# Attention of a head stage by stage for both halves, and the meta products of the next group in front of the present second quad, in a float32 convolution-and-retention trunk

## The chip, the cores and the metric

The kernel runs on one core of a Trainium2 chip. The metric is the device time of one execution in microseconds (us). The engines are TensorE (PE, matrix products into PSUM), VectorE (DVE), ScalarE (ACT), GpSimd (POOL) and SyncE (SP, which here issues all transfers between HBM and SBUF). Each engine runs its own queue in order; semaphores tie the queues together.

## The reference

One layer over 2048 tokens of width 1024, with 16 learned meta tokens ahead of them. Batch is 1, and all data is float32.

```python
hn = rms_norm(concat(meta, x), norm1_g)
cx, cb, cc, cg, q, k, v, rg = split(hn @ w_in, 8)          # 8 parts of 512 columns
conv_out = cb * causal_conv(cc * cx, conv_w) * silu(cg)    # 3 taps for each column
qf, kf = rotary(q) * 128 ** -0.5, rotary(k)                # 4 heads of 128 columns
ret = retention_chunkwise(qf, kf, v)                       # chunks of 128 tokens, a decayed state per head
ret_out = head_group_norm(ret, ret_norm_g) * silu(rg)
out = rms_norm(x + concat(conv_out, ret_out) @ w_out, final_g)   # the meta tokens' rows are dropped
```

In each head `retention_chunkwise` makes, chunk by chunk, the masked scores `q k^T` times `v` plus `q` times the state before the chunk, and updates the state with the decayed `k^T v`. The meta tokens matter in two ways alone: their `k` and `v` give each head's first state, and their `cc * cx` the two values that the convolution needs from before the first token.

## The kernel before

Work is laid out with columns of the projection on partitions and tokens along the free axis. The tokens are taken in two **rounds** (r) of 1024, each of two **halves** (j) of 512. Within a round come four heads (h), each a K,V group and a Q,RG group of projections, and then four convolution groups (g), each a CC,CX group and a CG,CB group. A group of projections is a **quad**: 2 x 2 blocks of output over the two halves and two blocks of the contraction. A quad is made in the Strassen-Winograd way with seven block products (L199 to L234). A float32 operand is split into a high and a low part (`wh`, `wl` for weights, `mh`, `ml` for tokens), and each block product is three times four matmuls 128x512 (L208), so a quad has 84 big products on PE. The first quads of a round and of the output are plain ones of 96 (L258). `take` then combines the banks on DVE and does what the group needs (rotation, gates).

The weights of a quad come in four blocks of 128x512 (tile `ra`, a ring of 8 that also serves POOL's sums `sa`). `stationary` (L121) makes the seven block sums on POOL, in place, and the splits on ACT (L99, `wh`) and DVE (L111, `wl`), in rings of 3. So a block's buffer comes free, and the load of a later block can start, only when DVE and POOL have used it.

A head's attention (from L563) takes one half after the other. For each half: transposes of `k` and `v` (L569, L574), scaled copies on ACT, the update products (L584), and four states in a row on DVE (L587). Then for each half: scores (L599), mask on DVE (L601), output products (L609, L610), statistics (L615, L617), the power on POOL (L622), the scaling (L626), transposes (L633), gate (L634) and store.

**The meta products.** In round 0, `ahead` (L711) loads the next group's first quad's blocks and also multiplies them with the 16 meta columns. That is L392: sixteen matmuls of 16x128 into four strips of one PSUM bank. For a head `meta_state` rotates the result on DVE, with a table `mr` that it loads itself, and `meta_update` makes the first state on PE (L420). For a convolution group `meta_carry` multiplies and transposes (L428). In before, `ahead` stands behind the present group's second quad, and `update` behind the first half's states.

PSUM has four banks for projections (`pj`) and four for all else (`ms`). The scratch of the meta products (`mk`), their table (`mr`) and the quads' copies (`tc`) share four buffers.

The order in which the instructions stand on each engine is not that of the code. The program is built with a scheduler that goes through the code's order with its own estimate of times and puts each instruction where its operands and buffers are estimated to be ready; the code's order sets the priority. So the attention of a head is spread between the big products of the following quads.

Of the kernel before, what the change touches and what calls it, by code (L numbers as in the profile page):

```python
# [14 lines left out]
P = 128  # L15
# [53 lines left out]
def hybrid_trunk(ctx: ExitStack, tc: tile.TileContext, t, out: bass.AP, chunk_decay):  # L69
# [316 lines left out]
    def meta_products(blocks):  # L386

        bank = ps_misc()
        four = [bank[i * 32 : i * 32 + NMETA, :P] for i in range(4)]
        for kt in range(KH):  # L390
            for i in range(4):
                nc.tensor.matmul(  # L392
                    four[i], meta_s[:, i % 2 * KH + kt, :], blocks[i][:, kt * P : (kt + 1) * P],
                    start=kt == 0, stop=kt == KH - 1,
                )
# [4 lines left out]
        nc.scalar.copy(out=d, in_=four[3])  # L400
        add(nc.vector, a, four[0], c)
        add(nc.vector, b, b, d)
        return a, b, c, d

    def meta_state(h, blocks):

        rot = sb.tile([P, HB], F32, name="mr", tag="tc", bufs=COPIES)[:NMETA, : 2 * P].rearrange("p (a c) -> p a c", a=2)
        nc.sync.dma_start(rot, t["rot_m"][h])
        k, v, a, b = meta_products(blocks)
        half = P // 2  # L410
        lo, hi = slice(0, half), slice(half, P)
        for i, j in ((lo, hi), (hi, lo)):
            nc.vector.tensor_tensor(out=b[:, i], in0=k[:, j], in1=rot[:, 1, i], op=ALU.mult)
        nc.vector.tensor_tensor(out=a, in0=k, in1=rot[:, 0], op=ALU.mult)
        add(nc.vector, k, a, b)
        return k, v

    def meta_update(h, k, v):
        up = ps_misc()
        nc.tensor.matmul(up[:, :P], k, v, start=True, stop=True)  # L420
        nc.scalar.copy(out=state[h], in_=up[:, :P])

    def meta_carry(g, blocks):

        cc, cx, u, _ = meta_products(blocks)
        nc.vector.tensor_tensor(out=u, in0=cc, in1=cx, op=ALU.mult)
# [33 lines left out]
    def conv_group(g, r, m, f, blocks, ahead):  # L460
# [8 lines left out]
        def take(i, j, pp, c):  # L469
# [45 lines left out]
    def head(h, r, m, rot_t, f, blocks, ahead, first=(), between=()):  # L515
# [6 lines left out]
        def take(i, j, pp, c):  # L522
# [8 lines left out]
            else:  # L531
                v[j] = d

        if len(first) > 0:
            quad_plain(first[0], m, take)
        else:
            quad(stationary(blocks), m, take)
# [19 lines left out]

        if len(first) > 1:
            quad_plain(first[1], m, take)
        else:  # L560
            quad(stationary(load_raw(w_loads(2 * h + 1))), m, take)
        next(between, lambda: None)()
        blocks, update = ahead()  # L563
        states = [state[h]]
        vt = []
        for j in range(2):
            tp = ps_misc()
            for c in range(CH):
# [3 lines left out]
            tp = ps_misc()  # L572
            for c in range(CH):
                nc.tensor.transpose(tp[:, c * P : (c + 1) * P], v[j][:, c * P : (c + 1) * P], ident)  # L574
            vj = v[j]
            for c in range(CH):
                cs = slice(c * P, (c + 1) * P)
                nc.scalar.mul(vj[:, cs], tp[:, cs], f[2][j][0][:, c : c + 1])
            vt.append(vj)
            last = r == NR - 1 and j == 1  # L580
            up = ps_misc()
            for c in range(CH - last):
                cs = slice(c * P, (c + 1) * P)
                nc.tensor.matmul(up[:, cs], kd[:, cs], vj[:, cs], start=True, stop=True)  # L584
            for c in range(CH - last):
# [5 lines left out]
                states.append(nxt)  # L591
            if j == 0:
                update()

        for j in range(2):
            sc = ps_misc()
            for c in range(CH):
# [6 lines left out]
                in1=causal.rearrange("p (c i) -> p c i", c=1).broadcast_to([P, CH, P]), op0=ALU.mult, op1=ALU.mult,  # L604
            )
            o = ps_misc()
            for c in range(CH):
                cs = slice(c * P, (c + 1) * P)
                nc.tensor.matmul(o[:, cs], pm[:, cs], vt[j][:, cs], start=True, stop=False)  # L609
                nc.tensor.matmul(o[:, cs], q[j][:, cs], states[j * CH + c], start=False, stop=True)  # L610

            st = small.tile([P, CH, 6], F32, name="st", tag="st")
# [9 lines left out]
            nc.gpsimd.tensor_tensor(out=rp, in0=rs, in1=neg_half.rearrange("p (c a) -> p c a", a=1), op=ALU.pow)  # L622
            y = pm
            for c in range(CH):
# [4 lines left out]
                )  # L629
            yT = ps_misc()  # L630
            for c in range(CH):
                cs = slice(c * P, (c + 1) * P)
                nc.tensor.transpose(yT[:, cs], y[:, cs], ident)  # L633
            nc.vector.scalar_tensor_tensor(  # L634
# [76 lines left out]
    def ahead(r, n):  # L711


        if n == 2 * NG:
            return None, lambda: None
# [11 lines left out]
    for r in range(NR):  # L727
# [7 lines left out]
        if r == 0:  # L735
# [10 lines left out]
            first = [[p for a, p in w]]  # L746
            k0, v0 = meta_state(0, [a for a, p in w])
            first.append(plain_parts(w_loads(1)))
# [19 lines left out]

            between = (lambda: meta_update(0, k0, v0), rest)
            later = prepare(load_x(1), sums_x, gain_of)  # L770
        else:
# [3 lines left out]
            prepared(m, sums_x, (1, 3))  # L775
            between = (lambda: prepared(m, sums_x, (0, 2)),)
            later = prepare(load_w_out, sums_w)
        blocks = None
        for h in range(NG):
# [5 lines left out]
        for g in range(NG):  # L785
            blocks = conv_group(g, r, m, f, blocks, lambda: ahead(r, NG + g + 1)[0])
            for _ in range(3):
                next(steps, None)
# [44 lines left out]
```

## Time and profile before

| | us |
|---|---|
| median of 3 runs (lowest, highest) | 910.4 (909.9, 913.95) |
| the profiled execution | 909.45 |
| its span, first to last instruction | 907.7 |
| PE, DVE, ACT, POOL busy | 887.2, 707.1, 405.1, 391.6 |

The mean granted TensorE clock is 0.996 of full speed. A row of the profile names line, engine, operation, output tile <- input tiles, shapes and count; then busy us, the mean in ns, and the idle time before with what ended it. A row of the timeline has start and duration in us, and in brackets how long the engine stood idle before it and what ended that. A matmul of full float32 operands other than a transpose shows as two records. Matmuls overlap, so the distance between starts tells more than a duration. In a table by stretches the columns are the stretch, its length, the busy time of PE, PE's weight loads, DVE, ACT and POOL (with counts), the granted clock, the share of the DMA engines and GB/s.

### The profile page before, as it was taken

Reading aid. Unit: us, or ns where it says so; the run is one execution under the profiler, and the core shown is the slowest. Engines: PE = TensorE matmul, PEld = TensorE weight load, DVE = VectorE, ACT = ScalarE, POOL = GpSimd, SP = SyncE. Lnnn points to the kernel's source line nnn. Section 1 sums busy time; section 2 is a strip of 40 time slices with the busy share of each in tenths; the row PEclk is TensorE's granted clock in tenths of the full one; section 3 lists DMA queues with packets and bytes.
Section 4 is the critical chain, followed back from the end, with each engine's and each line's share of the span. In section 5 each row is a group of like instructions: output and inputs, shape, how many; then the busy total and the mean of one; then the engine's idle time right before and its main releaser. Section 6 shows DMA issues by size and latency. Waiting matters only on the chain.

```text
span 907.7 us, 12870 instructions
## 1 busy us (share of the span) xinstructions
PE 887.2 (98%) x4407; PEld 726.4 (80%) x4407; DVE 707.1 (78%) x1177; ACT 405.1 (45%) x807; POOL 391.6 (43%) x290
## 2 busy tenths in 40 slices
PE   8999999999999999999999999999999999999996
PEld 5778878787886777878888888888888888788885
DVE  6699898997665665799888999877767698866764
ACT  8762242424343534565333242433333374554553
POOL 0133142322434645343333323435646554778773
PEclk9999999999999999999999999999999999999999
DMA  9801451623142323564126362222131585555532
GB/s 332 264 3 47 140 163 51 206 82 98 43 149 61 105 82 117 194 236 139 47 67 200 93 204 89 56 59 81 58 93 48 185 284 184 172 183 164 173 108 93
DMA packets 76242, 116.94 MB, mean 129 GB/s; under 512 B 7632, under 2 KB 24336, under 8 KB 76176
## 3 DMA queue, kind: packets, MB, share of 16 engines
q1 hardware_dynamic: 76176, 116.11, 40.0%
q8 instruction: 35, 0.57, 0.3%
q14 instruction: 31, 0.25, 0.1%
HBM read 90.92 MB, written 25.17 MB: 128 GB/s over the span
## 4 chain that ended last, share of the span: by engine, by line
PE 81%; DVE 9%; DMA 3%; ACT 3%; issue 2%; POOL 1%; SPq 0%; POOLq 0%; ACTq 0%; DVEq 0%
PE pj L208 65%; PE pj L258 6%; DVE wl L111 2%; DVE ml L111 1%; PE ms L609 1%; PE ms L610 1%; PE ms L599 1%; DMA ra<-in_x 1%; PE ms L584 1%; PE ms L392 1%; PE ms L633 1%; PE ms L569 1%; PE ms L574 1%; ACT mh L102 1%; DMA ra<-in_w_in 1%
## 5 line engine op out<-in xcount | busy, mean ns | idle before, releaser
L208 PE MATMUL pj<-mh,wl 128*128 128x512 f32 x1008 | 400.6, 398 | 4.8 <-DVE wl L111 3.7
L208 PE MATMUL pj<-ml,wh 128*128 128x512 f32 x1008 | 393.6, 390 | 1.1 <-DVE ml L111 1.1
L208 PE MATMUL pj<-mh,wh 128*128 128x512 f32 x1008 | 393.5, 390 | 0.0
L99 ACT CAST wh<-ra 128x512 fp32r<-128x512 f32 x216 | 133.8, 620 | 306.9 <-PE pj L208 255.3
L208 PEld LDWEIGHTS pj<-mh,wl 128*128 128x128 f32 x1008 | 189.6, 188 | 49.1 <-issue 3.4
L208 PEld LDWEIGHTS pj<-mh,wh 128*128 128x128 f32 x1008 | 189.4, 188 | 39.9
L208 PEld LDWEIGHTS pj<-ml,wh 128*128 128x128 f32 x1008 | 189.8, 188 | 39.0 <-DVE ml L111 1.4
L111 DVE TENSOR_TENSOR wl<-ra,wh 128x512 fp32r<-128x512 f32 x216 | 180.8, 838 | 49.0 <-ACT wh L99 48.4
L111 POOL TENSOR_TENSOR ra<-ra 128x512 f32<-128x512 f32 x72 | 111.9, 1554 | 78.9 <-issue 35.0
L108 POOL TENSOR_TENSOR sa<-ra 128x512 f32<-128x512 f32 x36 | 54.8, 1522 | 119.8 <-DVE wl L111 54.9
L111 POOL TENSOR_TENSOR ra<-sa,ra 128x512 f32<-128x512 f32 x36 | 54.2, 1506 | 107.2 <-DVE wl L111 106.8
L215 ACT COPY tc<-pj 128x512 f32<-128x512 f32 x108 | 62.7, 580 | 0.1
L258 PE MATMUL pj<-mh,ml 128*128 128x512 f32 x128 | 48.6, 394 | 2.6 <-ACT kv L525 1.9
L258 PE MATMUL pj<-ml,mh 128*128 128x512 f32 x128 | 50.2, 392 | 0.1
L258 PE MATMUL pj<-mh,mh 128*128 128x512 f32 x128 | 50.0, 395 | 0.0
L622 POOL TENSOR_TENSOR rp<-rs,neg_half 128x4 f32<-128x4 f32 x16 | 20.5, 1279 | 56.0 <-DVE rs L108 55.7
L467 POOL TENSOR_TENSOR c<-c,tc 128x512 f32<-128x512 f32 x16 | 28.9, 1805 | 34.4 <-ACT tc L490 34.4
L467 POOL TENSOR_TENSOR c<-c,rr 128x512 f32<-128x512 f32 x16 | 30.1, 1879 | 24.8 <-DVE c L455 13.0
L663 DVE TENSOR_TENSOR yo<-pj,yo 128x512 f32<-128x512 f32 x32 | 22.0, 688 | 19.4 <-POOL yo L108 10.1
L111 DVE TENSOR_TENSOR ml<-t,mh 128x512 fp32r<-128x512 f32 x40 | 35.3, 922 | 1.4 <-ACT mh L99 1.4
L108 DVE TENSOR_TENSOR tc<-pj,tc 128x512 f32<-128x512 f32 x32 | 22.0, 686 | 18.0 <-PE pj L208 18.0
L99 ACT CAST wh<-sa 128x512 fp32r<-128x512 f32 x36 | 22.3, 619 | 28.6 <-PE pj L208 28.2
(129 smaller groups left out, 1131.4 us busy)
## 6 DMA issues: line engine op xcount, KB each, us to landing
ra<-in_w_in SPq DMA_DIRECT2D x128, 256.0 KB, 2.7
x<-in_xT SPq DMA_DIRECT2D x48, 256.0 KB, 5.0
ra<-in_x SPq DMA_DIRECT2D x32, 256.0 KB, 3.5
w<-in_w_out SPq DMA_DIRECT2D x32, 256.0 KB, 5.3
ra<-mixed SPq DMA_DIRECT2D x32, 256.0 KB, 2.7
yo<-in_x SPq DMA_DIRECT2D x32, 256.0 KB, 4.3
mixed<-qg SPq DMA_DIRECT2D x16, 256.0 KB, 2.3
sums_x<-x SPq DMA_DIRECT2D x16, 256.0 KB, 2.7
```

Of the source, the lines that this page charges most:

```text
L99: nc.scalar.copy(out=hi, in_=src)
L102: nc.scalar.mul(hi, src, scale)
L108: eng.tensor_tensor(out=out, in0=a, in1=b, op=ALU.add)
L111: eng.tensor_tensor(out=out, in0=a, in1=b, op=ALU.subtract)
L208: nc.tensor.matmul(bank, a[:, ks], b, start=first and kt == 0 and n == 0, stop=kt == KH - 1 and n == 2, skip_group_check=not first,)
L215: nc.scalar.copy(out=c, in_=bank)
L258: nc.tensor.matmul(banks[i], a[:, ks], b, start=half + kt + n == 0, stop=half == 1 and kt == KH - 1 and n == 2,)
L392: nc.tensor.matmul(four[i], meta_s[:, i % 2 * KH + kt, :], blocks[i][:, kt * P : (kt + 1) * P], start=kt == 0, stop=kt == KH - 1,)
L467: eng.tensor_tensor(out=out, in0=a, in1=b, op=ALU.mult)
L569: nc.tensor.transpose(tp[:, c * P : (c + 1) * P], k[j][:, c * P : (c + 1) * P], ident)
L622: nc.gpsimd.tensor_tensor(out=rp, in0=rs, in1=neg_half.rearrange("p (c a) -> p c a", a=1), op=ALU.pow)
L663: last[0] = nc.vector.tensor_tensor(out=y, in0=pp, in1=y, op=ALU.add)
```

## The change

`ahead` is called ahead of the present group's second quad, and makes the next group's products and their copies by ACT there. They ask for the last block first (3, 2, 1, 0), and all four strips go to SBUF by ACT; the sums on DVE are now of SBUF alone. DVE's part and the state's product (`meta_state`, `meta_carry`) follow a quad later: behind the second quad of the head they belong to, or behind the first quad of the convolution group. The attention of a head does each stage for both halves before the next stage, and its transposes go from the last chunk to the first.

```diff
         for kt in range(KH):
-            for i in range(4):
+            for i in (3, 2, 1, 0):
                 nc.tensor.matmul(
...
-        a, b, c, d = (scratch[:NMETA, i] for i in range(4))
-        nc.scalar.copy(out=c, in_=four[1])
-        nc.scalar.copy(out=b, in_=four[2])
-        nc.scalar.copy(out=d, in_=four[3])
-        add(nc.vector, a, four[0], c)
-        add(nc.vector, b, b, d)
-        return a, b, c, d
+        for i in range(4):
+            nc.scalar.copy(out=scratch[:NMETA, i], in_=four[i])
+        return scratch
+
+    def meta_sums(scratch):
+        a, b, c, d = (scratch[:NMETA, i] for i in range(4))
+        add(nc.vector, a, a, b)
+        add(nc.vector, c, c, d)
+        return a, c, b, d
...
-        k, v, a, b = meta_products(blocks)
+        k, v, a, b = meta_sums(scratch)
...
-        return k, v
-
-    def meta_update(h, k, v):
         up = ps_misc()
         nc.tensor.matmul(up[:, :P], k, v, start=True, stop=True)
         nc.scalar.copy(out=state[h], in_=up[:, :P])
...
@@ conv_group
+        blocks, meta = blocks
         quad(stationary(blocks), m, take)
+        if meta:
+            meta_carry(g, meta)
         carry(u, g, r)
...
-        quad(stationary(load_raw(w_loads(n))), m, take)
+        w = stationary(load_raw(w_loads(n)))
         blocks = ahead()
+        quad(w, m, take)
...
@@ head
-        if len(first) > 1:
-            quad_plain(first[1], m, take)
-        else:
-            quad(stationary(load_raw(w_loads(2 * h + 1))), m, take)
+        w = first[1] if len(first) > 1 else stationary(load_raw(w_loads(2 * h + 1)))
+        blocks = ahead()
+        (quad_plain if len(first) > 1 else quad)(w, m, take)
         next(between, lambda: None)()
-        blocks, update = ahead()
-        states = [state[h]]
-        vt = []
-        for j in range(2):
+        if meta:
+            meta_state(h, meta)
+
+        def transposed(src):
             tp = ps_misc()
-            for c in range(CH):
-                nc.tensor.transpose(tp[:, c * P : (c + 1) * P], k[j][:, c * P : (c + 1) * P], ident)
+            for c in reversed(range(CH)):
+                nc.tensor.transpose(tp[:, c * P : (c + 1) * P], src[:, c * P : (c + 1) * P], ident)
+            return tp
+
+        kds = []
+        for j in range(2):
+            tp = transposed(k[j])
             kd = brief("kd")
             nc.scalar.mul(kd, tp, kd_col[:, h : h + 1])
-            tp = ps_misc()
...
+            kds.append(kd)
+        for j in range(2):
+            tp = transposed(v[j])
...
+        states = [state[h]]
+        for j in range(2):
             last = r == NR - 1 and j == 1
             up = ps_misc()
...
-            if j == 0:
-                update()
-
+        pms = []
         for j in range(2):
             sc = ps_misc()
...
+            pms.append(pm)
+        outs = []
+        for j in range(2):
             o = ps_misc()
...
+            outs.append(o)
+        for j in range(2):
+            o = outs[j]
...
+        for j in (1, 0):
+            yT = transposed(pms[j])
...
@@ ahead
-        if r == 0 and n < NG:
-            k, v = meta_state(n, blocks)
-            return blocks, lambda: meta_update(n, k, v)
-        if r == 0:
-            meta_carry(n - NG, blocks)
-        return blocks, lambda: None
+        return blocks, meta_products(blocks) if r == 0 else None
```

What this does to the order on the engines shows at three places.

PE, round 0, the fourth head's second quad and the start of the quad behind it: the meta products of the first convolution group (L392) among big products (L208, of which only neighbours are shown), with the transposes of the scaled output `pm` (L633, now L572). Before:

```order
L208 MATMUL pj<-mh_723,wh 128x512
L633 MATMUL ms<-ident,pm 128x128
L392 MATMUL ms<-ra,meta_s 16x128 x5
L633 MATMUL ms<-ident,pm 128x128 x3
L392 MATMUL ms<-ra,meta_s 16x128 x2
L208 MATMUL pj<-mh_234,wl 128x512
...
L392 MATMUL ms<-ra,meta_s 16x128 x3
...
L392 MATMUL ms<-ra,meta_s 16x128 x6
L208 MATMUL pj<-mh_115,wl 128x512
```

The same products in the changed order:

```order
L208 MATMUL pj<-mh_181,wh 128x512
L572 MATMUL ms<-ident,pm 128x128 x8
L208 MATMUL pj<-mh_715,wl 128x512
...
L208 MATMUL pj<-ml_724,wh 128x512
L392 MATMUL ms<-ra,meta_s 16x128 x16
L208 MATMUL pj<-mh_723,wh 128x512
```

Four pieces became one, some 50 big products further ahead. Over the whole program L392 stands in 24 places before and in 8 after, always as sixteen.

PE, round 0, third head's first quad: the meta update (L420, now L419), whose input `mk` DVE makes, between the update products of the head before (L584, now L592) and transposes (L569 and L574, now L572). Before:

```order
L392 MATMUL ms<-ra,meta_s 16x128 x15
L569 MATMUL ms<-ident,kv 128x128 x4
L574 MATMUL ms<-ident,kv 128x128 x4
...
L584 MATMUL ms<-kv,kd 128x128 x4
L420 MATMUL ms<-mk 128x128
L569 MATMUL ms<-ident,kv 128x128 x4
L574 MATMUL ms<-ident,kv 128x128 x4
```

In the changed order:

```order
L208 MATMUL pj<-mh_139,wh 128x512
L419 MATMUL ms<-mk 128x128
L572 MATMUL ms<-ident,kv 128x128 x12
...
L572 MATMUL ms<-ident,kv 128x128 x4
L208 MATMUL pj<-mh_181,wh 128x512
L592 MATMUL ms<-kv,kd 128x128 x4
```

Before, the third head's update stands here, 12 big products behind its own meta products. Now the second head's stands here, whose products are a quad and more back, ahead of the transposes of both halves of that head, which come in a row.

DVE, round 0, third head's attention during the fourth head's first quad: states (L587, now L595), masks (`pm`, L601, now L607), statistics (L615, now L626). Before:

```order
L601 SCALAR_TENSOR_TENSOR pm<-ms,cols,causal 128x512
L587 SCALAR_TENSOR_TENSOR state<-state,ms 128x128
L111 TENSOR_TENSOR wl<-ra,wh 128x512
L587 SCALAR_TENSOR_TENSOR state<-state,ms 128x128 x2
L108 TENSOR_TENSOR kv<-pj,tc 128x512
L111 TENSOR_TENSOR wl<-ra,wh 128x512
L615 BN_STATS st<-ms 128x6 x4
```

In the changed order:

```order
L607 SCALAR_TENSOR_TENSOR pm<-ms,cols,causal 128x512
L108 TENSOR_TENSOR kv<-kv,rot 128x512
L607 SCALAR_TENSOR_TENSOR pm<-ms,cols,causal 128x512
L595 SCALAR_TENSOR_TENSOR state<-state,ms 128x128 x3
L111 TENSOR_TENSOR wl<-ra,wh 128x512
L595 SCALAR_TENSOR_TENSOR state<-state,ms 128x128 x2
L108 TENSOR_TENSOR kv<-pj,tc 128x512
L111 TENSOR_TENSOR wl<-ra,wh 128x512
L626 BN_STATS st<-ms 128x6 x4
```

The second half's mask, which stood a quad later, is now next to the first half's, ahead of the last states.

More of the change, by code (lines that the diff above doesn't have):

```diff
@@ L421, in meta_update, with meta_carry @@
         nc.scalar.copy(out=state[h], in_=up[:, :P])
-    def meta_carry(g, blocks):
-        cc, cx, u, _ = meta_products(blocks)
+    def meta_carry(g, scratch):
+        cc, cx, u, _ = meta_sums(scratch)
         nc.vector.tensor_tensor(out=u, in0=cc, in1=cx, op=ALU.mult)
@@ L532, in take @@
                 v[j] = d
+        blocks, meta = blocks
         if len(first) > 0:
@@ L583, in head @@
                 cs = slice(c * P, (c + 1) * P)
-                nc.tensor.matmul(up[:, cs], kd[:, cs], vj[:, cs], start=True, stop=True)
+                nc.tensor.matmul(up[:, cs], kds[j][:, cs], v[j][:, cs], start=True, stop=True)
             for c in range(CH - last):
@@ L608, in head @@
                 cs = slice(c * P, (c + 1) * P)
-                nc.tensor.matmul(o[:, cs], pm[:, cs], vt[j][:, cs], start=True, stop=False)
+                nc.tensor.matmul(o[:, cs], pms[j][:, cs], v[j][:, cs], start=True, stop=False)
                 nc.tensor.matmul(o[:, cs], q[j][:, cs], states[j * CH + c], start=False, stop=True)
+            outs.append(o)
+        for j in range(2):
+            o = outs[j]
             st = small.tile([P, CH, 6], F32, name="st", tag="st")
@@ L629, in head @@
                 )
[L630 to L633, printed above, removed]
+        for j in (1, 0):
+            yT = transposed(pms[j])
             nc.vector.scalar_tensor_tensor(
@@ L746, in hybrid_trunk @@
             first = [[p for a, p in w]]
-            k0, v0 = meta_state(0, [a for a, p in w])
+            blocks = None, meta_products([a for a, p in w])
             first.append(plain_parts(w_loads(1)))
@@ L767, in rest @@
                         parts(m, i, kt, held[kt])
-            between = (lambda: meta_update(0, k0, v0), rest)
+            between = (lambda: None, rest)
             later = prepare(load_x(1), sums_x, gain_of)
@@ L776, in hybrid_trunk @@
             between = (lambda: prepared(m, sums_x, (0, 2)),)
+            blocks = None, None
             later = prepare(load_w_out, sums_w)
-        blocks = None
         for h in range(NG):
@@ L785, in hybrid_trunk @@
         for g in range(NG):
-            blocks = conv_group(g, r, m, f, blocks, lambda: ahead(r, NG + g + 1)[0])
+            blocks = conv_group(g, r, m, f, blocks, lambda: ahead(r, NG + g + 1))
             for _ in range(3):
```

14 lines of the change are left out of this document (5 added, 9 removed).

## The prediction

> **What bounds the kernel.** I read the busy shares first, then what TensorE (PE) waited for (total in us, times, longest), then the chain that ended last and PE's timeline.
>
> ```profile
> span 907.7 us, 12870 instructions
> PE 887.2 (98%) x4407; PEld 726.4 (80%) x4407; DVE 707.1 (78%) x1177; ACT 405.1 (45%) x807; POOL 391.6 (43%) x290
> ...
> PE pj L208 <- DVE wl L111: 3.7, 3, 1.7
> ...
> PE ms L420 <- DVE mk L108: 2.1, 1, 2.1
> ...
> PE ms L633 <- DVE pm L626: 0.3, 1, 0.3
> ```
>
> PE is busy 98% of the span, and the waits of it that the change can touch are few: 3.7, 2.1 and 0.3 us. The change has the same arithmetic, so it can gain in two ways only: the small products cost PE less because of where they stand, or waits go. Busy time doesn't price the first, since matmuls overlap; starts do. In the main stream a 128x512 product starts each 0.227 us, as a long piece of the chain without waits has it (start us, us, what):
>
> ```profile
> 620.02 103.42 PE pj L208 x456
> ```
>
> 103.42 / 456 = 0.227. A break in it costs the time from the last big start before it to the second big start behind it, less 2 x 0.227.
>
> First, an attention stage as a break:
>
> ```profile
> 148.06 0.39 PE L208 MATMUL pj<-mh,wh 128*128 128x512 f32 x1
> 148.28 0.38 PE L609 MATMUL ms<-kv,pm 128*128 128x128 f32 x2
> ...
> 149.84 0.39 PE L610 MATMUL ms<-state,qg 128*128 128x128 f32 x2
> 149.98 0.48 PE L208 MATMUL pj<-mh,wl 128*128 128x512 f32 x1
> 150.30 0.40 PE L208 MATMUL pj<-ml,wh 128*128 128x512 f32 x1
> ```
>
> 150.30 - 148.06 - 0.454 = 1.79 us for 16 records of 0.11 us: nothing beside the work itself. Whether attention's products stand in one group or in four is **free** on PE. Not so the meta products (16 rows of output, L392), here once as a whole and once as a single matmul:
>
> ```profile
> 57.99 0.39 PE L258 MATMUL pj<-mh,mh 128*128 128x512 f32 x1
> 58.31 1.07 PE L392 MATMUL ms<-ra,meta_s 128*16 128x128 f32 x32
> 59.30 0.50 PE L208 MATMUL pj<-mh,wl 128*128 128x512 f32 x1
> 59.64 0.40 PE L208 MATMUL pj<-ml,wh 128*128 128x512 f32 x1
> ...
> 284.13 0.39 PE L208 MATMUL pj<-mh,wh 128*128 128x512 f32 x1
> 284.45 0.39 PE L392 MATMUL ms<-ra,meta_s 128*16 128x128 f32 x2
> 284.78 0.50 PE L208 MATMUL pj<-mh,wl 128*128 128x512 f32 x1
> 285.11 0.39 PE L208 MATMUL pj<-ml,wh 128*128 128x512 f32 x1
> ```
>
> All sixteen: 59.64 - 57.99 - 0.454 = 1.20 us. One alone: 285.11 - 284.13 - 0.454 = 0.53 us. So a matmul of this kind costs (1.20 - 0.53) / 15 = 0.045 us, and **each break that holds some costs 0.48 us**.
>
> **Term 1, the meta products in one piece.** The eight groups' 128 products stand in 24 places in the order of before, and in 8 places of sixteen in that of the change, since their reversed order asks for the last block first. 16 places fewer x 0.48 = **-7.7 us**. Ends: -7.7, and 0 if PE must wait for the last block (first rival). Where a piece stands between transposes its break may cost a little less; I keep 0.48, the price of two rows.
>
> **Term 2, the wait of the meta update.** In the third head's first quad PE reaches the update before DVE has finished its input:
>
> ```profile
> 121.31 0.48 PE L420 MATMUL ms<-mk 16*128 16x128 f32 x2 [2.13 <-DVE mk L108]
> ...
> 121.70:125.10 3.40, 3.40 (x13) 3.09 (x13) 3.35 (x7) 2.09 (x6) 0.00 (x0) 0.50 0.32 98
> ```
>
> The wait is 2.13 us, and behind it the granted clock stands at 0.50 for 3.4 us, which loses half of that, 1.7 us. The change takes the products a quad earlier and DVE's sums and rotation behind that quad. PE meets the update at least 57 big products (13 us) behind the products. I take **-3.8 us**. Ends: -3.8, and 0 if the update waits as long for its table. That table (`mr`) is now asked for late, by a load that waits for DVE's take of the quad's product 4:
>
> ```profile
> DMA to landing us min/median/max: 1.5/2.3/4.9
> ...
> L414 DVE TENSOR_TENSOR mk<-mk,mr 16x128 f32<-16x128 f32 x4 | 2.2, 544 | 0.0
> L413 DVE TENSOR_TENSOR mk<-mk,mr 16x64 f32<-16x64 f32 x8 | 2.5, 344 | 0.0
> L108 DVE TENSOR_TENSOR mk<-mk 16x128 f32<-16x128 f32 x12 | 7.7, 646 | 0.0
> L108 DVE TENSOR_TENSOR mk<-ms,mk 16x128 f32<-16x128 f32 x8 | 2.2, 278 | 7.9 <-ACT mk L400 7.9
> ```
>
> From that take, DVE has 0.7 (take) + 2.3 (landing) + 2 x 0.34 + 0.54 + 0.65 = 4.9 us to the update's input. PE has 24 products of this quad and 9 of the next before it, 33 x 0.227 = 7.5 us. With a landing of 4.9 it is just met. Queued behind the waiting DVE instruction are a `qg` sum and the second conversion of the next quad, 12 products later still. Behind `mr` on SP's queue stand loads for the next round.
>
> The Trainium skill (TensorE: Matmul & The Clock Gate, section HAM oscillation — how this bites in real kernels) gives as its abstract rule no TensorE gap over about 3.4 us. By that the wait would cost 2.1 us alone and the sum below would be 1.7 us smaller; the trace differs, with a clock of 0.50 behind a gap of 2.13 us, and the trace decides.
>
> **Term 3, the second meta carry.** At 272 us the sums of the next group stand on DVE ahead of the weights' conversion that PE needs:
>
> ```profile
> 272.35 1.33 DVE L426 TENSOR_TENSOR mk<-mk 16x128 f32<-16x128 f32 x1
> 273.85 0.69 DVE L108 TENSOR_TENSOR u<-pj,tc 128x512 f32<-128x512 f32 x1 [0.17 <-PE pj L208]
> ...
> 274.52 0.91 DVE L111 TENSOR_TENSOR wl<-ra,wh 128x512 fp32r<-128x512 f32 x1
> ...
> 275.49 0.50 PE L208 MATMUL pj<-mh,wl 128*128 128x512 f32 x1 [1.46 <-DVE wl L111]
> ```
>
> In the change these sums follow a quad later, behind two conversions: **-1.5 us**, ends 0 and -1.5.
>
> **Term 4, the second head's first quad.** POOL's weight sums there stood idle for the meta products, and PE later for a conversion:
>
> ```profile
> 59.55 2.18 POOL L111 TENSOR_TENSOR ra<-ra 128x512 f32<-128x512 f32 x1 [11.34 <-PE ms L392]
> ...
> 67.64 0.47 PE L208 MATMUL pj<-mh,wl 128*128 128x512 f32 x1 [1.70 <-DVE wl L111]
> ```
>
> The products now stand 15 big products (3.4 us) earlier, so POOL starts earlier; but DVE was also busy with rotations there. Ends 0 and -1.7; I take the middle, **-0.9 us**.
>
> **Term 5, what is added.** Eight more ACT copies of a bank's quarter lie on an engine that is busy 45% of the span. Eight DVE sums read SBUF alone instead of PSUM: 646 against 278 ns, 2.9 us in all. Over one head DVE has 7 us free (44.34 of 51.30 busy, the third pair):
>
> ```profile
> 134.20:185.50 51.30, 51.30 (x292) 42.03 (x290) 44.34 (x88) 18.73 (x39) 14.85 (x11) 1.00 0.42 134
> L111 DVE TENSOR_TENSOR wl<-ra,wh 128x512 fp32r<-128x512 f32 x216 | 180.8, 838 | 49.0 <-ACT wh L99 48.4
> L587 DVE SCALAR_TENSOR_TENSOR state<-state,ms 128x128 f32<-128x128 f32 x60 | 16.9, 282 | 4.0 <-PE ms L584 3.1
> L601 DVE SCALAR_TENSOR_TENSOR pm<-ms,cols,causal 128x512 f32<-128x512 f32 x16 | 11.9, 745 | 0.0
> DVE pm L626 <- POOL rp L622: 12.9, 14, 2.2
> ```
>
> That cover is thinner at one place. Stage by stage, both halves' states and masks must be done before the second half's output products. Between scores and outputs the third and fourth head have 22 big products, 5.0 us; DVE's rows there are 2 x 0.745 (masks), 5 x 0.282 (states), a conversion (0.84) and a rotation's sum of the same shape (taken as 0.84 too), 4.6 us. So 0.4 us is left, and a late DVE shows on PE. No row of before has this form; the nearest is PE's wait of 0.3 us on the attention's `pm`, and I take that for each of the eight heads: **+2.4 us**. Ends: 0, and 8 x 2.7 = 21.6 us: a head's two waits of DVE for POOL's `rp`, one the longest (2.2) and one the mean (12.9 / 14 = 0.9), both on PE's path, less the 0.4.
>
> The Trainium skill (SBUF — State Buffer, section SBUF: two separate sides) speaks against moving the sums to SBUF: a DVE operation with both inputs there is locked out while GpSimd reads SBUF. The rows of 646 and 278 ns agree; with eight sums exposed on PE the sum would be 2.9 us worse, which DVE's free 7 us a head hide.
>
> **Sum.** -7.7 - 3.8 - 1.5 - 0.9 + 2.4 = -11.5 us, a span of 896.2. The profiled execution took 909.45 us, 1.75 more than its span, and 0.95 under the median of 910.4 (909.9 to 913.95). So 896.2 + 1.75 = **898.0 us**, own range 894 to 902.
>
> **Rivals.**
> *The one piece waits for its last block.* In the order of before the early pieces went out as blocks landed. In the change PE, in order, holds all until the fourth has landed, and that load waits for DVE and POOL in the present second quad.
>
> ```profile
> 275.59 17.34 SPq L432 DMA_DIRECT2D ra<-in_w_in  x5
> ...
> DMA to landing us min/median/max: 2.6/2.7/3.7
> ...
> 296.51 0.77 PE ms L392 x20
> ```
>
> The fifth load was issued by 292.9, landed by 295.6, and was needed at 296.5: 0.9 us to spare. At six groups (not the first two) a block later by 2 us would cost 6 x 1.1 = 7 us: 905 us. For it: the thin margin; against: the piece stands at the same product of the quad as the fourth block's first use did.
>
> *The breaks cost nothing.* If the 0.48 us is only a slip of PE's pipeline that the big products behind make up, the change doesn't do what it says on PE: -3.8 - 1.5 - 0.9 + 2.4 = -3.8, 905.6 us. Against: 456 products in a row without a wait still take 0.227 us each, so the stream has no faster step in which to make anything up.
>
> *DVE's bunches make PE wait: slower.* The mechanism is that of term 5, at the output products of every head: eight times 2.7 us instead of 0.3 gives 21.6 - 13.9 = +7.7, 917 us. It decides from 1.7 us a head on; from 2.4 us a head it is slower by over 0.5%. For it: 0.4 us of cover; against: in before the same engines gave 0.3 us in 16 half heads.
>
> **Chances.** The forecast has 0.62, a still better sum (under 894) 0.04, late blocks 0.13, free breaks 0.12, DVE's bunches 0.09. Half of the two middle cases lies below 905.9, the bound of 0.5%, about the least that a measurement of this kernel tells from no change. So faster 0.78, same 0.13, slower 0.09. The range 893 to 907 takes in the forecast and the two rivals near 905 and leaves out the slower one.
>
> **What would show it.** Term 1: L392 stands in eight pieces of 32 records and each takes 1.2 us between big starts. Term 2: the meta update (now L419) without a wait and no stretch of 0.50 near it. Term 3 and 4: no wait of PE for L111 near the second carry and in the second head. Term 5: PE's waits for the masks, states or `rp` sum to some 2 us. Wrong would be the forecast if PE waits before L392 for a load, if the rows behind a piece start closer than 0.227, or if PE waits over 1.7 us a head for DVE.

## The result, and the profile after

| | before | after |
|---|---|---|
| median of 6 runs each, us (lowest, highest) | 910.92 (909.9, 913.95) | 925.74 (924.24, 930.62) |
| ratio to before, 95% interval | | 1.0166 (1.0139 to 1.0193) |
| the profiled execution, its span | 909.45, 907.7 | 930.62, 928.7 |
| mean granted TensorE clock | 0.996 | 0.983 |

The change made the kernel 15 us slower; 11.5 us faster was forecast. The profiled execution of after is the slowest of its six, 4.9 us over their median, so its rows show causes and places, and sizes are taken from ratios where there is one.

The page's head and PE's waits of after (total in us, times, longest):

```profile
span 928.7 us, 12865 instructions
PE 891.4 (96%) x4407; PEld 732.8 (79%) x4407; DVE 709.2 (76%) x1177; ACT 407.7 (44%) x815; POOL 385.3 (41%) x290
...
PE pj L208 <- ACT tc L215: 15.1, 11, 3.6
PE pj L208 <- DVE wl L111: 4.5, 2, 3.9
PE ms L572 <- DVE pm L637: 2.4, 1, 2.4
```

The same wait in before:

```profile
PE pj L208 <- ACT tc L215: 0.9, 2, 0.6
```

PE is busy for about as long as before (891 against 887 us) and the span is 21 us longer: PE waits. The new wait is one that the prediction never named. Before a product into a bank that has been used, ACT must have copied the bank out (`tc`, L215): 0.9 us in before, 15.1 now. Setting the starts of the same big products of both executions side by side, after is 18.4 us behind when the second round begins (product 1344 of 3408, at 389.49 us in before and at 407.89 in after). So nearly all of it is lost in round 0, where the meta work lies.

One such place, the third head's second quad, on PE and then on ACT, with ACT at the same quad of before as the third view:

```profile
161.35 0.39 PE L208 MATMUL pj<-ml,wh 128*128 128x512 f32 x1
161.67 1.07 PE L392 MATMUL ms<-ra,meta_s 128*16 128x128 f32 x32
162.66 0.50 PE L208 MATMUL pj<-mh,wh 128*128 128x512 f32 x1
163.00 0.40 PE L208 MATMUL pj<-mh,wl 128*128 128x512 f32 x1
...
163.47 0.40 PE L208 MATMUL pj<-mh,wh 128*128 128x512 f32 x1
164.57 0.50 PE L208 MATMUL pj<-mh,wl 128*128 128x512 f32 x1 [0.71 <-ACT tc L215]
...
167.20 0.39 PE L208 MATMUL pj<-mh,wh 128*128 128x512 f32 x1
168.78 0.50 PE L208 MATMUL pj<-mh,wl 128*128 128x512 f32 x1 [1.19 <-ACT tc L215]
```

```profile
156.35 0.62 ACT L99 CAST wh<-sa 128x512 fp32r<-128x512 f32 x1 [1.61 <-PE pj L208]
159.07 0.62 ACT L99 CAST wh<-ra 128x512 fp32r<-128x512 f32 x1 [2.10 <-PE pj L208]
162.83 1.08 ACT L398 COPY mk<-ms 16x128 f32<-16x128 f32 x4 [3.13 <-PE ms L392]
163.93 0.59 ACT L215 COPY tc<-pj 128x512 f32<-128x512 f32 x1
...
168.15 1.07 ACT L215 COPY tc<-pj 128x512 f32<-128x512 f32 x2
```

```profile
145.75 0.62 ACT L99 CAST wh<-sa 128x512 fp32r<-128x512 f32 x1 [2.98 <-PE pj L208]
146.27 0.58 ACT L215 COPY tc<-pj 128x512 f32<-128x512 f32 x1
...
166.74 0.26 ACT L398 COPY mk<-ms 16x128 f32<-16x128 f32 x1 [3.21 <-PE ms L392]
```

The copy of 163.93 is that of product 0 (numbered as in `quad`, from 0). Products 0 and 1 lie ahead of transposes that start at 158.88, so the first bank was complete some 12 x 0.227 us before these, at about 156.3, and its copy came 7.6 us later. In before the copy stands right behind the conversion `wh<-sa` (0.5 us), and the meta copies come 20 us after it. ACT was not busy in between: it idled for 2.10 us ahead of another conversion and then for 3.13 us, waiting for the meta products, since the four meta copies (`mk`) now stand ahead of the bank copy in its queue. The Trainium skill (PSUM — Partial Sum Buffer, section Engine vs sequencer instructions) calls ScalarE's queue strictly first in, first out; the trace agrees.

The late copy has also turned the quad's own order round. The built programs give it (x is the bank of products 0, 2, 4 and 6, y that of 1, z that of 3 and 5):

```
before:  x(0) y(1) x(2) z(3) x(4) z(5) x(6)
after:   x(0) y(1) z(3) x(2) x(4) z(5) x(6)
```

With product 3 ahead of 2, products 2 and 4 stand one behind the other in the same bank, and the copy between them (`u2`) lies on PE's path: the second wait, 167.20 to 168.78. Seven of the 14 quads of round 0 have that order: the second quads of heads two to four and of the first three convolution groups, and the second head's first quad. No quad of before has it. The traces agree: in after seven pairs of bank copies stand back to back (as at 168.15) in round 0, in before none.

In the convolution groups ACT has more in front of that copy. ACT and PE in the first group, and the stretch behind:

```profile
267.01 0.59 ACT L215 COPY tc<-pj 128x512 f32<-128x512 f32 x1
267.49 0.63 ACT L317 ACTIVATE ra<-ra 128x512 f32<-128x512 f32 x1
...
270.08 0.63 ACT L317 ACTIVATE ra<-ra 128x512 f32<-128x512 f32 x1 [1.87 <-DMA ra<-in_x]
...
273.42 0.63 ACT L317 ACTIVATE ra<-ra 128x512 f32<-128x512 f32 x1 [0.95 <-DMA ra<-in_x]
...
274.55 1.06 ACT L215 COPY tc<-pj 128x512 f32<-128x512 f32 x2
```

```profile
275.18 0.50 PE L208 MATMUL pj<-mh,wl 128*128 128x512 f32 x1 [3.56 <-ACT tc L215]
```

```profile
273.00:283.00 10.00, 7.82 (x27) 6.34 (x28) 3.68 (x5) 4.49 (x11) 4.94 (x6) 0.83 0.40 131
```

ACT squares rows of the next round (L317) and waits for their loads with the copy of 274.55 queued behind. PE stands for 3.56 us, and the granted clock is 0.83 over the ten us from 273. At 0.50 a product starts each 0.427 us instead of 0.227. Between 50 and 700 us 38 starts of after are 0.40 to 0.45 us apart (called half-clock starts below) and 3 of before, 0.2 us lost at each: 7.0 us more.

### The profile page after: what moved, and what is told of

The parts are those of the page before. It is cut to its first block, busy times and chain, and to the rows that moved or that the text cites. A ratio compares the mean times of both kernels' runs of the same rounds, so it can differ in the third digit from the quotient of the medians.

```text
span 928.7 us, 12865 instructions
## 1 busy us (share of the span) xinstructions
PE 891.4 (96%) x4407; PEld 732.8 (79%) x4407; DVE 709.2 (76%) x1177; ACT 407.7 (44%) x815; POOL 385.3 (41%) x290
## 4 chain that ended last, share of the span: by engine, by line
PE 76%; DVE 5%; ACT 3%; DMA 3%; issue 1%; SPq 0%; POOLq 0%; POOL 0%; ACTq 0%; DVEq 0%
PE pj L208 64%; PE pj L258 5%; PE ms L572 2%; DMA ra<-in_x 2%; DVE wl L111 1%; PE ms L592 1%; PE ms L605 1%; PE ms L619 1%; PE ms L618 1%; ACT tc L215 1%; ACT wh L99 1%; DVE ml L111 1%; DMA x<-in_xT 1%; ACT ra L317 0%; DVE w L111 0%
## 5 line engine op out<-in xcount | busy, mean ns | idle before, releaser
L208 PE MATMUL pj<-mh,wl 128*128 128x512 f32 x1008 | 402.5, 400 | 19.8 <-ACT tc L215 15.1
L208 PE MATMUL pj<-ml,wh 128*128 128x512 f32 x1008 | 396.8, 394 | 1.1 <-DVE ml L111 1.1
L208 PE MATMUL pj<-mh,wh 128*128 128x512 f32 x1008 | 397.7, 395 | 0.0
L208 PEld LDWEIGHTS pj<-mh,wl 128*128 128x128 f32 x1008 | 191.6, 190 | 64.6 <-ACT tc L215 20.9
L111 DVE TENSOR_TENSOR wl<-ra,wh 128x512 fp32r<-128x512 f32 x216 | 189.0, 877 | 50.6 <-ACT wh L99 50.3
L208 PEld LDWEIGHTS pj<-mh,wh 128*128 128x128 f32 x1008 | 191.6, 190 | 40.9 <-issue 0.4
L208 PEld LDWEIGHTS pj<-ml,wh 128*128 128x128 f32 x1008 | 192.0, 191 | 39.8 <-DVE ml L111 1.4
L111 POOL TENSOR_TENSOR ra<-sa,ra 128x512 f32<-128x512 f32 x36 | 52.2, 1449 | 144.1 <-DVE wl L111 144.0
L215 ACT COPY tc<-pj 128x512 f32<-128x512 f32 x108 | 62.2, 583 | 1.7 <-DVE ml L111 1.6
L108 POOL TENSOR_TENSOR yo<-yo,tc 128x512 f32<-128x512 f32 x21 | 31.3, 1493 | 7.0 <-ACT tc L215 6.2
```

The lines of the kernel that those rows point to most:

```text
L108: eng.tensor_tensor(out=out, in0=a, in1=b, op=ALU.add)
L111: eng.tensor_tensor(out=out, in0=a, in1=b, op=ALU.subtract)
L208: nc.tensor.matmul(bank, a[:, ks], b, start=first and kt == 0 and n == 0, stop=kt == KH - 1 and n == 2, skip_group_check=not first,)
L215: nc.scalar.copy(out=c, in_=bank)
```

## The experiments

My theory after the two traces, **shared buffers**: the copies of a quad and the meta copies take turns at four buffers (`tc`, COPIES = 4), in the order of the code. With the meta products ahead of the second quad, their copies stand ahead of that quad's, ACT runs them in that order, and the order of the products follows. Rivals: **attention** (DVE's bunches of the stage-by-stage attention, the prediction's slower rival) and **place** (products ahead and DVE's part behind cost by themselves). Ratios are to before on the same chip.

**The meta part alone**, with the attention code of before:

```diff
-        kds = []
-        for j in range(2):
-            tp = transposed(k[j])
...
+        states = [state[h]]
+        vt = []
+        for j in range(2):
+            tp = ps_misc()
+            for c in range(CH):
+                nc.tensor.transpose(tp[:, c * P : (c + 1) * P], k[j][:, c * P : (c + 1) * P], ident)
...
```

> The change's meta part alone: products and their copies ahead of the second quad, sums, rotation and update behind it; the attention is that of before, half by half. Theory 'shared buffers': the meta copies take one of the four buffers that the quad's own bank copies use, and take it ahead of them, so ScalarE copies the first bank only behind the meta copies, the fourth product is put ahead of the third and PE waits at the bank twice in a quad; seven quads of the first round have that order here as in the change, so 921 to 928 us, with PE's wait for the bank copies (L215) at 10 to 17 us. Rival 'attention': the loss is DVE's bunches of the stage-by-stage attention, which are gone here, so 900 to 911 us and the bank waits under 5 us.

932.55 us, ratio 1.0242 (1.0219 to 1.0265); PE's waits for L215 are 17.4 us. The time is above the expected 921 to 928. The seven reordered quads are there. The loss is all in the meta part, and more than in the whole change.

**The attention alone**, with the meta part of before:

```diff
-        blocks = ahead()
-        (quad_plain if len(first) > 1 else quad)(w, m, take)
...
+            quad(stationary(load_raw(w_loads(2 * h + 1))), m, take)
+        next(between, lambda: None)()
+        blocks, update = ahead()
...
+            if j == 0:
+                update()
```

> The change's attention alone, stage by stage for both halves, with the meta products, sums and update placed as before. 'Shared buffers': no quad has its fourth product ahead of its third, so 906 to 914 us and PE's waits for the bank copies near before's 0.9 us. 'Attention': 918 to 928 us, with PE waiting 8 to 15 us for DVE's masks, states or normalised rows.

908.39 us, ratio 0.9988 (0.9976 to 0.9999), no quad reordered. PE's waits:

```profile
PE pj L208 <- ACT tc L215: 2.7, 6, 0.7
PE pj L208 <- DVE wl L111: 2.5, 2, 1.9
...
PE ms L616 <- DVE pm L605: 0.6, 1, 0.6
```

For the masks and the like PE waits 0.6 us in all. "Attention" falls: stage by stage costs nothing, and gains about 1 us (the interval almost reaches 1).

**Buffers of their own** for the meta copies. There was room for two narrow ones:

```diff
-        scratch = sb.tile([P, HB], F32, name="mk", tag="tc", bufs=COPIES).rearrange("p (a c) -> p a c", a=CH)
+        scratch = sb.tile([P, 2 * P], F32, name="mk", tag="mk", bufs=2).rearrange("p (a c) -> p a c", a=2)
+        quarters = [scratch[i // 2 * 32 : i // 2 * 32 + NMETA, i % 2] for i in range(4)]
...
-        return sb.tile([P, HB + 128], F32, name=name, tag="b", bufs=BRIEF)[:, :HB]
+        return sb.tile([P, HB], F32, name=name, tag="b", bufs=BRIEF)[:, :HB]
```

> The change with the meta copies in two buffers of their own (a narrower tile, room for it from the unused columns of the masks' tile); everything else stays where the change puts it. 'Shared buffers': the bank copies no longer queue behind the meta copies, no quad has the changed order of products, and the 15 us of waits for L215 and most of the half-clock stretches behind them go: 898 to 910 us. Rival 'place': products ahead and DVE's part behind are late or early by themselves whatever their buffer: 918 us or more. 'Attention': 918 us or more too.

901.93 us, ratio 0.9918 (0.9899 to 0.9937). No quad is reordered. PE's waits between 60 and 420 us, and ACT at the same quad as above:

```profile
PE pj L208 <- DVE kv L108: 1.6, 2, 0.8
PE ms L621 <- DVE state L597: 1.1, 3, 0.7
PE pj L208 <- DVE wl L111: 1.0, 1, 1.0
PE pj L208 <- ACT tc L215: 0.4, 1, 0.4
```

```profile
146.36 0.58 ACT L215 COPY tc<-pj 128x512 f32<-128x512 f32 x1
...
152.31 1.08 ACT L399 COPY mk<-ms 16x128 f32<-16x128 f32 x4 [3.13 <-PE ms L392]
```

The meta copies still wait 3.13 us for their products, but product 0's copy now stands 6 us ahead of them. The bank waits of this stretch, 13.9 us in after, are 0.4; 7 half-clock starts are left of 38. The ratio falls by 0.025, 23 us. "Shared buffers" is right, "place" falls. This version beats both kernels.

**The copies alone behind**: products ahead, their bank held, ACT's copies moved behind the quad.

```diff
-        for i in range(4):
-            nc.scalar.copy(out=scratch[:NMETA, i], in_=four[i])
-        return scratch
+        return four

-    def meta_sums(scratch):
+    def meta_sums(four):
+        scratch = sb.tile([P, HB], F32, name="mk", tag="tc", bufs=COPIES).rearrange("p (a c) -> p a c", a=CH)
+        for i in range(4):
+            nc.scalar.copy(out=scratch[:NMETA, i], in_=four[i])
```

> The change with only the four meta copies moved: the products stay ahead of the second quad, their bank is held, and ScalarE's copies stand behind that quad, at the sums. 'Shared buffers': the quad's own copies take their buffers first, so 898 to 910 us and PE's waits for L215 under 3 us. 'Place' and 'attention': 918 us or more.

902.3 us, ratio 0.9919 (0.9903 to 0.9935), without a byte more of SBUF. PE's waits for L215 are 2.4 us. The tag is shared as before; only the turn is different. So the turn is what cost the time.

**The order alone.** Is it the late copy or the turned order that costs? First before, with that order forced on the same seven quads:

```diff
+        swapped = next(quads) in (0, 1, 3, 5, 7, 9, 11)
...
+        if swapped:
+            zb = ps_proj()
+            p3 = product(3, zb, True)
+            c3 = copy(zb)
+        with tc.issue_after(p3.ins) if swapped else nullcontext():
+            product(2, xb, False)
...
+        with tc.issue_after(p4.ins) if swapped else nullcontext():
+            product(5, zb, False)
```

> The kernel before, in which seven quads of the first round (the same seven as in the change) issue the fourth product ahead of the third and the sixth behind the fifth, so that the third and fifth, both into the first bank, stand one behind the other; buffers and meta work as before. If that order alone costs what the trace of the change shows at its second wait, 7 x 1.35 us (1.58 between two starts less 0.23), the time is about 9 us above before, less some 2 us for five pieces of meta products fewer: 915 to 920 us, with L215 waits of 7 to 10 us. If the order is harmless while the first copy is in time, 906 to 912 us.

921.32 us, ratio 1.0108 (1.0082 to 1.0135): more than 920, and not for the reason expected. The waits for the copy are 12.2 us, but in 4 places, not 7. All four are in the convolution groups or behind them. The first, on PE and on ACT (the squares are L330 here, the copies L220, the big products L212):

```profile
261.79 0.79 PE L212 MATMUL pj<-mh,wl 128*128 128x512 f32 x1 [4.60 <-ACT tc L220]
```

```profile
256.68 0.63 ACT L330 ACTIVATE ra<-ra 128x512 f32<-128x512 f32 x1 [2.33 <-DMA ra<-in_x]
...
260.03 0.63 ACT L330 ACTIVATE ra<-ra 128x512 f32<-128x512 f32 x1 [1.12 <-DMA ra<-in_x]
...
261.17 0.57 ACT L220 COPY tc<-pj 128x512 f32<-128x512 f32 x1
```

In the heads there is none. At the third head's second quad the copy of product 2's bank (153.94 to 154.52) runs while PE does transposes of the attention and meta products (153.57 to 156.47) ahead of product 4. In the convolution groups ACT is held up by the squares' loads, and with product 2 next to 4 nothing covers that. The order costs by what ACT has in front of the copy: nothing to 4.6 us, and half clock behind.

**The order held.** The change, with product 3 forced to stay behind product 2:

```diff
-        product(2, xb, False)
+        p2 = product(2, xb, False)
...
-        product(3, zb, True)
+        with tc.issue_after(p2.ins):
+            product(3, zb, True)
```

> The change with one thing held: the fourth product may only be issued behind the third, so no quad has the changed order; the meta copies still share the quad's buffers. If the order alone is the loss, its second waits go (7 x 1.35 us and some half clock) and the time is 908 to 916 us. If the late first copy is the cause, PE now comes to the third product 12 products earlier and waits there for the same copy, which still stands behind the meta copies: L215 waits of 15 us or more in all, 925 to 940 us.

925.09 us, ratio 1.0156 (1.0135 to 1.0178): as slow as the change. PE, and ACT, at the third head's second quad (lines are shifted by one or two):

```profile
159.39 1.07 PE L394 MATMUL ms<-ra,meta_s 128*16 128x128 f32 x32 [0.25 <-DMA ra<-in_w_in]
162.29 0.50 PE L208 MATMUL pj<-mh,wl 128*128 128x512 f32 x1 [1.83 <-ACT tc L216]
```

```profile
160.55 1.08 ACT L400 COPY mk<-ms 16x128 f32<-16x128 f32 x4 [1.62 <-PE ms L394]
161.65 0.59 ACT L216 COPY tc<-pj 128x512 f32<-128x512 f32 x1
```

```profile
PE pj L208 <- ACT tc L216: 16.6, 10, 3.9
```

In the code's order PE comes to product 2 at once, finds product 0's bank not copied, and waits through the four meta copies. Six of the ten waits are of this kind, 1.83 us each; the longest, 3.9 us at 67.61 in the second head's first quad, is for a copy that waited for DVE. At the third head's second quad the turned order costs about the same (0.71 + 1.19 us in after). That the whole times are equal is in part luck. In the profiled execution of order_held PE also waits 4.8 us for `pm` at 102.92 (2.4 in after), with half clock behind; it is 15.6 us behind before at product 300 and 14.2 at product 1344, where after is 7.2 and 18.4 behind. So the late copy costs about as much without the turned order, and left to itself the order turns only where the meta copies are asked for ahead of the quad's in the same buffers (after and meta_alone, seven quads each). The cause is the late copy; that the scheduler turned the order to get round it is my reading, and no run shows its reasons.

**What a break costs.** own_buffers, asking for the first block first:

```diff
-            for i in (3, 2, 1, 0):
+            for i in range(4):
```

> As own_buffers, but the meta products ask for the first block first, as in the kernel before: 18 pieces of meta products in PE's order instead of 8. If each break that holds some costs 0.48 us, 10 x 0.48 = 4.8 us more than own_buffers: 905 to 908 us. If breaks are free, the time of own_buffers, 901 to 903 us, or less, since early pieces don't wait for the last block.

905.16 us, ratio 0.9932 (0.9916 to 0.9948). A piece of one matmul, in the third convolution group:

```profile
276.90 0.39 PE L208 MATMUL pj<-mh,wh 128*128 128x512 f32 x1
277.22 0.39 PE L392 MATMUL ms<-ra,meta_s 128*16 128x128 f32 x2
277.55 0.50 PE L208 MATMUL pj<-mh,wl 128*128 128x512 f32 x1
277.88 0.39 PE L208 MATMUL pj<-ml,wh 128*128 128x512 f32 x1
```

277.88 - 276.90 - 0.454 = 0.53 us, as in before. The profiled execution is 4.2 us longer than that of own_buffers (904.7 against 900.5), near the 4.8 of ten breaks, but it is the slowest of its six; the ratios differ by only 0.0014 (1.3 us), within their intervals. Side by side the two executions are level at product 900 (274.4 and 274.2 us) and 4.3 us apart at product 1344: the difference comes in the convolution groups, with six of the ten breaks. Pieces cost on PE what the rows say; how much of it the whole time keeps is open between these two.

**The table in its own buffer.** own_buffers left a wait at the first head's meta update. Here `mr` gets a buffer:

```diff
-        rot = sb.tile([P, HB], F32, name="mr", tag="tc", bufs=COPIES)[:NMETA, : 2 * P].rearrange("p (a c) -> p a c", a=2)
+        rot = sb.tile([P, 2 * P], F32, name="mr", tag="mr", bufs=1)[:NMETA].rearrange("p (a c) -> p a c", a=2)
```

Room for it comes from unused columns of the `gen` tiles and two buffers of `rs_v`.

> As own_buffers, with the rotation table of the meta rows in a buffer of its own too, so that its load needn't wait for one of the quad's copies. DVE waited 5.6 us for that load in own_buffers, and PE 2.6 us at the first meta update with some 1.7 us of half clock behind it. If the table is what made the update late, up to 4.3 us less: 897 to 900 us; if DVE's own queue did (conversions ahead of the rotation), the time of own_buffers, 901 to 903 us.

902.73 us, ratio 0.9912 (0.9893 to 0.9931): no different. The table's first load is now issued at 18.8 us and the update doesn't wait, but PE waits 3.8 us for `wl`, 3.2 of it at once. DVE is busy for 17.6 of the 18 us from 52 to 70 us. So the wait came back at another instruction.

**The first head's meta state early**, where before has it; the other seven as in own_buffers:

```diff
-            blocks = None, meta_products([a for a, p in w])
+            blocks = None, None
+            k0, v0 = meta_state(0, meta_products([a for a, p in w]))
```

> own_buffers with the first head's meta sums, rotation and update where the kernel before has them, ahead of the round; the other seven groups as in own_buffers. Over the first 66 us own_buffers loses 4 us against before, with a wait of 2.6 us at that update and 1.7 us of half clock. If that place is the cause, 897 to 900 us. If DVE is full there whatever stands first (own_table lost its gain to other waits), 901 to 904 us.

904.16 us, ratio 0.9926 (0.9914 to 0.9939): no gain in the whole time. The wait at the update is gone, and at product 210 this execution is 4.3 us ahead of that of own_buffers (61.4 against 65.7 us). Behind it PE waits 2.1 us for DVE at 64.15 and 1.8 us for ACT at 67.50, with half clock from 65.6 to 72.4, and at product 300 it is 1.7 us behind (97.5 against 95.8). DVE is busy for 17.8 of the 18 us from 52 to 70 us. Together with own_table: place and table do set the wait at the update, but without it another wait comes a few us later; what would help DVE there wasn't tried.

**Controls.** Before with own_buffers' two buffers; own_buffers with the attention of before; own_buffers with the products behind the quad (`meta_products` called after `quad`, on the blocks loaded ahead of it).

> The kernel before with the same two buffers for the meta copies as own_buffers, nothing else. If sharing hurts only where the meta copies are asked for ahead of a quad's copies, which before never does, the time of before within 2 us: 908 to 913 us. If own_buffers gained because the quads have a fourth buffer free, 901 to 906 us.

911.25 us, ratio 1.0003 (0.9993 to 1.0013): a buffer more is worth nothing to before.

> own_buffers with the attention of before, half by half: the change's meta part alone, cured. PE's order has 15 pieces of meta products (8 in own_buffers). If the two parts add up, 1.3 us of the attention and 7 x 0.48 = 3.4 us of breaks more than own_buffers: 905 to 908 us. If stage by stage costs PE waits for DVE's bunches, as the prediction's slower rival has it, below own_buffers: 896 to 901 us.

909.4 us, ratio 0.9988 (0.9976 to 1.0), above both expected ranges. The meta part alone gains about as little as the attention alone, and the two together 0.0082. They don't add up; without the attention's new order the meta products stand in 15 pieces (8 in own_buffers), and PE waits again for an update and a carry:

```profile
PE ms L429 <- DVE mk L427: 3.1, 1, 3.1
...
PE ms L420 <- DVE mk L108: 2.2, 1, 2.2
```

> own_buffers with the meta products behind the second quad in the program's text, their blocks loaded ahead as before; PE's order has 14 pieces instead of 8. If the gain is the pieces, 6 x 0.48 = 2.9 us more than own_buffers: 904 to 907 us. If standing ahead costs (the whole piece waits for its last block), below own_buffers: 897 to 901 us.

905.71 us, ratio 0.9944 (0.993 to 0.9957), 14 pieces. So standing ahead gains about 0.0026 (2.4 us; the intervals overlap a little), once it no longer holds up the quad's copies.

## Why the prediction was wrong

- **The step that failed** is the first sentence of term 5: "Eight more ACT copies of a bank's quarter lie on an engine that is busy 45% of the span." They were costed at nothing because ACT is idle half the time. But a share of busy time says nothing of a queue: the four copies of a group wait for products that come late, and the bank copies behind them wait too. copies_behind moves nothing but these copies and turns 1.0166 into 0.9919. I had seen that `mr` takes its turn at the quads' buffers and followed that to a load; I didn't follow `mk`, nor compare the order of the big products of before and after, which had turned in seven quads.
- **Term 1** (-7.7): right in the trace. In after each of the six pieces that stand between big products takes 1.2 us (161.35 to 163.00 less 0.454). In before the last two groups stand in five pieces each, which the rows put at 0.53 (three times), 0.97 and 0.53, 3.09 us for a group against 1.20 in one piece: 0.47 a break. It was drowned. In the ratios a piece is worth less than 0.48 us: ten cost 0.0014, six 0.0026.
- **Terms 2 and 3** (-3.8, -1.5): the waits named are gone from after. But own_buffers, which is free of the late copies, has a wait of 2.6 us and half clock at the first head's update, so term 2 was moved rather than won.
- **Term 4** (-0.9): wrong. The wait for `wl` in the second head's first quad (68.74 us in after) grew from 1.70 to 3.9 us, with 12 half-clock starts behind it. POOL did start its sums earlier (55.93 instead of 59.55), but DVE is busy for 12.9 of the 13 us between 56 and 69 us in after, and the conversion came late all the same.
- **Term 5's price and its rival**: attention_alone has 0.6 us of such waits, own_buffers 1.1 (for the states), against the 2.4 of the sum. The 2.4 us for `pm` in after stand at one place (105.44) and aren't in own_buffers. The slower rival had the right sign and the wrong mechanism.
- **The rival of the last block** decided nothing: only in order_held did the meta products wait for a load, twice, 0.5 us in all.
- With the late copies out of the way, own_buffers gains 7.5 us of the 11.5 that were forecast (0.0082 x 911); its 902 us would have lain in the range. It is won late: set beside before, the profiled execution of own_buffers is level at product 700 (219 us in both), about where the convolution groups begin, and 8.7 us ahead at product 1344, so those groups give all of it. At the start it goes from 3.7 us ahead at product 126 (37.1 us) to 2.9 behind at product 300 (95.8 us). That isn't the change's own: before_own goes from 2.9 ahead to 4.3 behind over the same products. Why the heads keep nothing of terms 1 and 2 stays open.

## What to carry to other kernels

Before work is moved ahead, list the buffers and queues that it shares with what it passes: a tile of a shared tag takes its turn where the code asks for it, and an in-order engine then holds all later copies until the earlier one's input is there. "The engine is half idle" is no cover for that; look at what stands behind the moved instruction in its queue, and at whether the order of the main stream itself has turned. And give a rarely used tile buffers of its own, or ask for it where it is ready.

## What the runs showed of the hardware

- **Half clock after shorter waits than I had counted on.** The 1.83 us wait of order_held at 162.29 is followed by a mean clock of 0.83 over the ten us behind (seven half-clock starts):

```profile
162.00:172.00 10.00, 9.71 (x36) 7.83 (x37) 5.45 (x8) 2.45 (x5) 0.56 (x1) 0.83 0.23 72
```

  The same execution has six waits of 1.83 us: three have seven half-clock starts behind them (162.29, 267.98, 353.78), two have none (215.94, 311.24), and the sixth (108.53) falls into half clock that began before it. After the three waits of 1.19 in after there is none. The waits of 2.6 to 4.6 us ahead of big products had 5 to 13 half-clock starts each. So a wait of 3.56 us, at 275.18 in after, costs 1.4 us more (seven starts). The Trainium skill (TensorE: Matmul & The Clock Gate, section HAM oscillation — how this bites in real kernels) puts the limit at gaps of about 3.4 us; here the trace has half clock from about half of that, though not behind every such wait.
- **A wait is cheap or dear by what stands next to it.** The same order of products cost no wait in the heads of order_alone, where transposes and meta products stood between products 2 and 4 (the one at 153.57 to 156.47), and up to 4.6 us in the convolution groups.
